# First layer of a split-float32 MLP: weight sums one pair ahead, activation sums on VectorE, two row tiles kept from PSUM, two bank tags

## The chip, the cores and the metric

One core of a Trainium2 chip runs the whole program. The metric is the device time of one execution in microseconds (us); smaller is better. The engines are TensorE (PE), VectorE (DVE), ScalarE (ACT), GpSimd (POOL) and SyncE (SP), of which the last only issues transfers here.

## The reference

One residual block over a sequence of 1024 rows with model width 1024: two kinds of attention, an output projection, and an MLP with squared relu. The change lies in the MLP's first layer and in what feeds it.

```python
        merged = gate_sb * (y_sb @ w_sb_out[l]) + gate_diff * (y_diff @ w_diff_out[l])
        x = x + rms_norm(merged @ w_o[l], g_post_mix[l])

        h = rms_norm(x, g_pre_mlp[l])
        u = jnp.square(jax.nn.relu(h @ w_up[l]))
        x = x + rms_norm(u @ w_down[l], g_post_mlp[l])
```

h is 1024 x 1024, u is 1024 x 4096, and everything is float32.

## The kernel before

**Products.** A float32 factor is split into a high and a low part (`split`, L606: ScalarE casts the high part at L607, VectorE subtracts to get the low part at L608), and a product takes three matmuls for each block of 128 rows. `product` (L755 to L767, matmul in L764) multiplies a 512-wide weight block with a page of h: 4 blocks x 3 = 12 matmuls of 128x512.

**First layer.** h is cut into a 2x2 arrangement of blocks, and the layer is done with seven block products instead of eight (Strassen's scheme in Winograd's form). The h pages are B11, B21, B22 and the differences T1 to T4. The weights come in 16 pairs of 128-column tiles (`up_pair(n)`, n = 0 to 15). For each pair, `sums` (L722) loads two tiles of `w_up` and GpSimd forms four sums of 128x512 (L726 to L729); `split_sums` then splits the results w1, w24, w32 into high and low parts. Pairs 4 to 15 also split the pair's own block wa and do seven products. For pairs 0 to 3 (AHEAD) the B11 and B21 products (`c11_0` to `c11_3`) are run ahead, before the other h pages exist; these pairs do five products later. VectorE adds the products out of PSUM (v, q, u12, u21, u22), ScalarE applies relu and square (`relu2`, L770 and L771). Then four activation sums us12 and us34 are formed on GpSimd (L866 to L869), and all seven parts are stored in DRAM for the second layer (L873; sums through SyncE's queue, the others through ScalarE's).

**What feeds it.** `finish_tile(t)`, t = 0 to 7, projects 128 rows, normalises them twice on ScalarE and VectorE (or_t, xr_t), transposes the result on TensorE (trh_t) and stores it in DRAM as h. Tile 7 alone goes from PSUM straight into the buffers `hraw`, as last 128 columns (LATE) of the blocks with c = 1; `load_h` reads the rest (EARLY, and the c = 0 blocks) back from DRAM when all tiles but 7 have been stored. The T pages are formed by subtractions of hraw on VectorE.

**Second layer.** It runs seven groups of products (L935), first A11 with B11: `load_a` reads activations, `load_b` weights of w_down, GpSimd subtracts weights (t, L900).

**Buffers and order.** Buffers come from pools with a fixed count for each tag: `row` 4, `raw` 2, `wide`, `tmp` 2, and two PSUM banks for each of the tags acc, sc, av, tr. A new tile of a tag waits until the last reader of the oldest one is done. Each engine executes its instructions in one fixed order, which a scheduler chooses at build time; each queue is in order too.

## Time and profile before

| | us |
|---|---|
| median of the runs | 1488.52 |
| fastest and slowest run | 1484.34, 1489.57 |
| the profiled execution | 1482.92 |
| its span, first to last instruction | 1481.2 |
| TensorE busy (matmuls) | 1442.6, 97% |
| VectorE busy | 959.9, 65% |
| ScalarE busy | 742.8, 50% |
| GpSimd busy | 406.4, 27% |

The page gives shares over the whole span. TensorE's gaps are short and lie in a few places, so the views by stretch and the timelines of single engines are of more use. In a timeline, a row is an instruction (or a run of like ones, with its count), and the bracket at its end gives how long the engine was idle before it and who released it.

### The profile page before, as it was taken

How to read it: one execution, taken by the hardware profiler on the slowest of the kernel's cores; microseconds unless marked ns; L12 is line 12 of the kernel's file. 1: busy time of each engine (PE TensorE's matmuls, PEld its weight loads, DVE VectorE, ACT ScalarE, POOL GpSimd, SP SyncE). 2: the span in 40 equal slices, each digit the busy share in tenths (PEclk: the TensorE clock that was granted, in tenths of full speed). 3: DMA queues.
4: the chain of work that ended last, by engine and by line, in shares of the span. 5: the costliest groups of instructions: out<-in, count | busy, mean ns of one | idle time of the engine just before them, and what ended most of it. 6: DMA issues, size and time to landing. Idle time of an engine off the chain costs nothing.

```text
span 1481.2 us, 20077 instructions
## 1 busy us (share of the span) xinstructions
PE 1442.6 (97%) x7302; PEld 1222.0 (83%) x7302; DVE 959.9 (65%) x1404; ACT 742.8 (50%) x1350; POOL 406.4 (27%) x376
## 2 busy tenths in 40 slices
PE   7999999999999999999999888999999999999997
PEld 6888998899889888888888766887888788888886
DVE  5487988898778857536554485444444489664783
ACT  6456666676556545744344363444445244534450
POOL 2022322230000000000001227655665557232611
PEclk9999999999999999999999999999999999999999
DMA  5342213222322344644367725344456585668671
GB/s 203 79 130 65 72 44 82 76 58 64 84 77 76 98 151 148 203 139 147 124 199 226 243 97 174 135 157 143 152 182 211 189 291 190 199 219 283 208 284 57
DMA packets 94459, 220.51 MB, mean 149 GB/s; under 512 B 9260, under 2 KB 25880, under 8 KB 94360
## 3 DMA queue, kind: packets, MB, share of 16 engines
q1 hardware_dynamic: 78904, 198.78, 41.6%
q10 hardware_dynamic: 15456, 20.45, 3.8%
q8 instruction: 57, 0.93, 0.3%
q14 instruction: 42, 0.34, 0.1%
HBM read 152.59 MB, written 60.57 MB: 144 GB/s over the span
## 4 chain that ended last, share of the span: by engine, by line
PE 80%; issue 7%; POOL 5%; DVE 3%; DMA 2%; ACT 1%; SPq 0%; POOLq 0%; DVEq 0%; ACTq 0%
PE dS L935 12%; PE dA L935 8%; PE o L656 6%; PE mix L567 6%; PE acc_gate L198 4%; PE acc_gate L196 4%; PE acc_gate L197 4%; PE c L764 3%; PE p_av L764 3%; PE p_tr L764 3%; PE z L263 2%; PE z L262 2%; PE tr_sb L281 2%; PE p_sc L764 1%; PE tr_df L281 1%
## 5 line engine op out<-in xcount | busy, mean ns | idle before, releaser
L331 DVE TENSOR_TENSOR_SCAN rest<-rest 128x896 f32<-128x896 f32 (+3 forms) x64 | 87.6, 1374 | 20.7 <-POOL rest L326 20.3
L198 PE MATMUL acc_gate<-h_hi,lo_gate 128*128 128x512 f32 x256 | 101.0, 394 | 0.0
L196 PE MATMUL acc_gate<-h_hi,hi_gate 128*128 128x512 f32 x256 | 100.8, 394 | 0.0
L197 PE MATMUL acc_gate<-h_lo,hi_gate 128*128 128x512 f32 x256 | 100.7, 393 | 0.0
L326 POOL TENSOR_SCALAR_AFFINE_SELECT rest<-rest 128x128 f32<-128x128 f32 x64 | 23.5, 367 | 240.5 <-ACT rest L322 223.8
L608 DVE TENSOR_TENSOR lS_lo<-raw_S,lS_hi 128x1024 fp32r<-128x1024 f32 x32 | 59.7, 1866 | 38.5 <-ACT lS_hi L607 38.3
L608 DVE TENSOR_TENSOR w_lo<-raw_up,w_hi 128x1024 fp32r<-128x1024 f32 x32 | 44.1, 1388 | 52.5 <-ACT w_hi L607 45.7
L935 PE MATMUL dS<-rT_hi,lS_hi 128*128 128x512 f32 x192 | 74.7, 389 | 0.0
L935 PE MATMUL dS<-rT_lo,lS_hi 128*128 128x512 f32 x192 | 74.7, 389 | 0.0
L935 PE MATMUL dS<-rT_hi,lS_lo 128*128 128x512 f32 x192 | 74.7, 389 | 0.0
L607 ACT CAST lS_hi<-raw_S 128x1024 fp32r<-128x1024 f32 x32 | 33.7, 1052 | 78.5 <-DMA raw_S<-s_dramS 50.0
L567 PE MATMUL mix<-y,hi_mix 128*128 128x512 f32 x256 | 68.6, 389 | 0.0
L116 POOL TENSOR_SCALAR rstd_o<-s 128x1 f32<-128x1 f32 x8 | 2.4, 299 | 239.7 <-DVE wa_lo L608 212.2
L394 ACT ACTIVATE s<-s,low 128x896 f32<-128x896 f32 (+7 forms) x64 | 49.6, 776 | 29.9 <-DVE low L389 29.7
L375 POOL MEMSET bias<- 64x64 f32 x4 | 0.6, 145 | 214.7 <-DMA bias<-bias_rows 154.6
L764 PE MATMUL c<-hB_hi,wa_hi 128*128 128x512 f32 x128 | 50.5, 395 | 7.8 <-ACT u L770 4.1
L389 DVE CUSTOM_DVE_ANT_0 s<-z,bias 128x512 f32<-128x512 f32 (+3 forms) x64 | 37.0, 587 | 32.3 <-PE z L263 26.4
L726 POOL TENSOR_TENSOR s<-raw_up 128x512 f32<-128x512 f32 x16 | 24.4, 1527 | 117.2 <-DMA raw_up<-in_w_up_dram 87.5
L567 PEld LDWEIGHTS mix<-y,hi_mix 128*128 128x128 f32 x256 | 48.0, 188 | 10.0
L198 PEld LDWEIGHTS acc_gate<-h_hi,lo_gate 128*128 128x128 f32 x256 | 48.1, 188 | 9.2
L770 ACT ACTIVATE u<-u 128x512 f32<-128x512 f32 x48 | 29.6, 628 | 51.9 <-DVE u L852 24.5
L197 PEld LDWEIGHTS acc_gate<-h_lo,hi_gate 128*128 128x128 f32 x256 | 48.2, 188 | 8.8
(339 smaller groups left out, 4871.4 us busy)
## 6 DMA issues: line engine op xcount, KB each, us to landing
raw_up<-in_w_up_dram SPq DMA_DIRECT2D x32, 512.0 KB, 4.2
s_dramS<-us SPq DMA_DIRECT2D x64, 256.0 KB, 2.5
raw_S<-s_dramS SPq DMA_DIRECT2D x32, 512.0 KB, 4.4
s_dramA<-u ACTq DMA_DIRECT2D x48, 256.0 KB, 2.6
raw_A<-s_dramA SPq DMA_DIRECT2D x24, 512.0 KB, 3.7
raw_gate<-in_w_in_dram SPq DMA_DIRECT2D x16, 512.0 KB, 3.7
gate_dram<-gt SPq DMA_DIRECT2D x32, 256.0 KB, 2.5
y<-y_dram SPq DMA_DIRECT2D x16, 512.0 KB, 7.0
```

The lines of the kernel that those rows point to most:

```text
L196: nc.tensor.matmul(acc, w_hi[:, ks], h_hi[k][:, cs], start=(k == 0), stop=False)
L197: nc.tensor.matmul(acc, w_hi[:, ks], h_lo[k][:, cs], start=False, stop=False)
L198: nc.tensor.matmul(acc, w_lo[:, ks], h_hi[k][:, cs], start=False, stop=(k == NK - 1))
L281: nc.tensor.transpose(tr[:, i * P:(i + 1) * P], w[qi][:, kb * P:(kb + 1) * P], ident)
L331: nc.vector.tensor_tensor_scan(back, back, back, 1.0, op0=ALU.mult, op1=ALU.bypass)
L389: nc.vector.tensor_tensor_reduce(out=s[:, c0:c1], in0=z, in1=bias[:, S - nk + c0:S - nk + c1], scale=1.0, scalar=BIG if prev is None else ...
L394: e = nc.scalar.activation(s[:, :nk], s[:, :nk], AF.Exp, bias=low, scale=-1.0, accum_out=sums[:, m:m + 1],)
L567: nc.tensor.matmul(accs[i][c], st[:, ks], mv[:, cs], start=(first and k % 4 == 0), stop=(last and k % 4 == 3),)
L608: nc.vector.tensor_tensor(lo, raw, f32(hi), op=ALU.subtract)
L656: nc.tensor.matmul(accs[n], st, mv[:, n * HALF:(n + 1) * HALF], start=(first and k == 0), stop=(last and k == NK - 1),)
L764: nc.tensor.matmul(acc, st[:, ks], mv, start=(first and k == 0 and i == 0), stop=(k == 3 and i == 2), skip_group_check=True,)
L935: nc.tensor.matmul(acc, st[:, e, ts], mv[:, e, :], start=(first and e == 0 and i == 0), stop=(last and e == 1 and i == 2))
```

## The change

1. `sums(n + 1)` is called in `up_pair(n)`, after the split of pair n's weights. Odd pairs load into two `row` tiles, even ones into two `raw` tiles as before.
2. The four activation sums go from GpSimd to VectorE; the third is placed ahead of the second.
3. Tile 6 goes from PSUM into `hraw` too, as tile 7 does; the transposes of tiles 6 and 7 and their copies come after `load_h`, which now leaves out 256 columns.
4. `c11_2` and `c11_3` use the bank tag "sc" instead of "acc".
5. Of the second layer's first two B11 weight blocks, one is loaded ahead into a `raw` tile, where two were loaded into `row` tiles.

```diff
-        if t == NT - 1:
-            load_h()
...
+        return partial(store_h, t, c, ts, o)
+
+    def store_h(t, c, ts, o):
...
-            if t == NT - 1:
+            if t >= NT - 2:
                 for q in range(2):
-                    nc.scalar.copy(hraw[j, 1, q][:, :, LATE], tr[:, q * 256:(q + 1) * 256].rearrange("p (k t) -> p k t", k=2))
+                    nc.scalar.copy(hraw[j, 1, q][:, :, ts], tr[:, q * 256:(q + 1) * 256].rearrange("p (k t) -> p k t", k=2))
...
+    FROM_DRAM = slice(0, HALF - 2 * P)
...
-                cs = EARLY if c else slice(0, HALF)
+                cs = FROM_DRAM if c else slice(0, HALF)
...
-    def sums(n, s1):
-        f0, f1 = (raw_up(2 * n + i, f"up{n}_{i}") for i in range(2))
+    def sums(n, s1=None):
+        if n % 2:
+            f0, f1 = (row(f"up{n}_{i}") for i in range(2))
+            for i, f in enumerate((f0, f1)):
+                nc.sync.dma_start(out=f, in_=w_up[2 * n + i])
+        else:
+            f0, f1 = (raw_up(2 * n + i, f"up{n}_{i}") for i in range(2))
+        if s1 is None:
+            s1 = row(f"s1_{n}", [P, HALF])
...
-        finish_tile(t)
+        finish = finish_tile(t)
+        if t < NT - 2:
+            finish()
+        elif t == NT - 2:
+            finish6 = finish
+        else:
+            load_h()
+            finish6()
+            finish()
...
-        accs = [bank("acc", f"c11_{2 * i + e}") for e in range(2)]
+        accs = [bank(BANKS[i % 2], f"c11_{2 * i + e}") for e in range(2)]
...
-        wa, w1, w24, w32 = weights0 if n == 0 else split_sums(*sums(n, row(f"s1_{n}", [P, HALF])))
+        wa, w1, w24, w32 = weights0 if n == 0 else split_sums(*summed)
+        summed = sums(n + 1) if n < UP - 1 else None
...
-        nc.gpsimd.tensor_tensor(s1, u12, u22, op=ALU.add)
-        nc.gpsimd.tensor_tensor(s2, s1, u11, op=ALU.subtract)
-        nc.gpsimd.tensor_tensor(s3, u11, u12, op=ALU.subtract)
-        nc.gpsimd.tensor_tensor(s4, u21, s2, op=ALU.subtract)
+        nc.vector.tensor_tensor(s1, u12, u22, op=ALU.add)
+        nc.vector.tensor_tensor(s3, u11, u12, op=ALU.subtract)
+        nc.vector.tensor_tensor(s2, s1, u11, op=ALU.subtract)
+        nc.vector.tensor_tensor(s4, u21, s2, op=ALU.subtract)
...
-            b11, b12 = first_b[pp] if pp < 2 else load_b(0, 0, pp, "a"), load_b(0, 1, pp, "a")
+            b11, b12 = first_b[0] if pp == 0 else load_b(0, 0, pp, "a"), load_b(0, 1, pp, "a")
...
-    first_b = [load_b(0, 0, pp, "a") for pp in range(2)]
+    first_b = [raw_tile("b00_first", [P, 2, HALF])]
+    nc.sync.dma_start(out=first_b[0], in_=wd[0, 0, 0])
```

TensorE, the products run ahead of the pairs. hB110 and hB111 are the halves of page B11, hB210 of B21; c11_i belongs to pair i. Before, the end of c11_0's first product and what follows it:

```order
L764 MATMUL c11_0_8928<-hB111_hi_8539,wa_lo0_8261 128x512
L764 MATMUL c11_1_8929<-hB110_hi_8537,wa_hi1_8266 128x512
L764 MATMUL c11_1_8929<-hB110_lo_8538,wa_hi1_8266 128x512
L764 MATMUL c11_1_8929<-hB110_hi_8537,wa_lo1_8267 128x512
L764 MATMUL c11_1_8929<-hB110_hi_8537,wa_hi1_8266 128x512
```

The same place after:

```order
L781 MATMUL c11_0_8926<-hB111_hi_8539,wa_lo0_8261 128x512
L781 MATMUL c11_2_8982<-hB110_hi_8537,wa_hi2_8272 128x512
L781 MATMUL c11_2_8982<-hB110_lo_8538,wa_hi2_8272 128x512
L781 MATMUL c11_2_8982<-hB110_hi_8537,wa_lo2_8273 128x512
L781 MATMUL c11_2_8982<-hB110_hi_8537,wa_hi2_8272 128x512
L781 MATMUL c11_2_8982<-hB110_lo_8538,wa_hi2_8272 128x512
L781 MATMUL c11_2_8982<-hB110_hi_8537,wa_lo2_8273 128x512
L781 MATMUL c11_2_8982<-hB111_hi_8539,wa_hi2_8272 128x512
L781 MATMUL c11_1_8927<-hB110_hi_8537,wa_hi1_8266 128x512
L781 MATMUL c11_1_8927<-hB110_lo_8538,wa_hi1_8266 128x512
```

Seven matmuls of c11_2 now stand between c11_0 and c11_1; before, c11_2 began only after both products of c11_0 and c11_1.

VectorE, around tile 7's last normalisation (or_7, the scalar-tensor-tensor that reads rstd_x27). hrawjcq is a block of h; L801 and L819 are the same subtraction. Before:

```order
L670 TENSOR_TENSOR or_7_8892<-o_7_1_8826,grow0_8169 128x512
L671 SCALAR_TENSOR_TENSOR xr_7_8891<-or_7_8892,rstd_o7_8897,xr_7_8891 128x1024
L676 SCALAR_TENSOR_TENSOR or_7_8892<-xr_7_8891,rstd_x27_8906,grow1_8171 128x1024
L801 TENSOR_TENSOR hraw000_8877<-hraw010_8875,hraw000_8877 128x2x384
L608 TENSOR_TENSOR hB220_lo_9052<-hraw110_8879,hB220_hi_9051 128x2x384
L803 TENSOR_TENSOR hraw010_8875<-hraw110_8879,hraw010_8875 128x2x384
```

After:

```order
L668 TENSOR_TENSOR or_7_8860<-o_7_1_8810,grow0_8169 128x512
L669 SCALAR_TENSOR_TENSOR xr_7_8859<-or_7_8860,rstd_o7_8865,xr_7_8859 128x1024
L819 TENSOR_TENSOR hraw000_8880<-hraw010_8878,hraw000_8880 128x2x384
L821 TENSOR_TENSOR hraw010_8878<-hraw110_8882,hraw010_8878 128x2x384
L819 TENSOR_TENSOR hraw001_8888<-hraw011_8886,hraw001_8888 128x2x384
L674 SCALAR_TENSOR_TENSOR or_7_8860<-xr_7_8859,rstd_x27_8874,grow1_8171 128x1024
L608 TENSOR_TENSOR hB220_lo_9050<-hraw110_8882,hB220_hi_9049 128x2x384
```

Three subtractions, one of them on a block of the second half (hraw001), have moved ahead of the normalisation that tile 7's transposes read.

GpSimd, sums of pairs 1 to 3 (s1_n and raw_up or up: weights; us12, us34: activations). Before:

```order
L728 TENSOR_TENSOR raw_up2_0_9336<-s1_2_9335,raw_up2_0_9336 128x512
L729 TENSOR_TENSOR raw_up2_0_9336<-raw_up2_0_9336 128x512
L866 TENSOR_TENSOR us12_1_9322<-u1_1_9241,u2_1_9242 128x512
L868 TENSOR_TENSOR us34_1_9323<-u11_0_8926,u1_1_9241 128x512
L867 TENSOR_TENSOR us12_1_9322<-us12_1_9322,u11_0_8926 128x512
L869 TENSOR_TENSOR us34_1_9323<-u2_1_9242,us12_1_9322 128x512
L726 TENSOR_TENSOR s1_3_9449<-raw_up3_1_9452 128x512
L727 TENSOR_TENSOR raw_up3_1_9452<-raw_up3_0_9450,raw_up3_1_9452 128x512
```

After:

```order
L737 TENSOR_TENSOR raw_up2_0_9239<-s1_2_9243,raw_up2_0_9239 128x512
L738 TENSOR_TENSOR raw_up2_0_9239<-raw_up2_0_9239 128x512
L735 TENSOR_TENSOR s1_3_9357<-up3_1_9354 128x512
L736 TENSOR_TENSOR up3_1_9354<-up3_0_9353,up3_1_9354 128x512
L737 TENSOR_TENSOR up3_0_9353<-s1_3_9357,up3_0_9353 128x512
L738 TENSOR_TENSOR up3_0_9353<-up3_0_9353 128x512
```

Between the weight sums of one pair and those of the next there is no longer an activation sum of the pair before.

## Rows read from the trace of the kernel before

**Rows 1.** Per-core line: span and mean granted TensorE clock
```profile
core 0: 1481.2 us, clock 0.995
```

**Rows 2.** Chain that ended last, in time order: start, us, what
```profile
836.80 3.41 DMA h_dram<-ht
...
1031.88 2.72 PE p_sc L764 x12
...
1172.10 3.89 DMA b_a<-in_w_down_dram
```

**Rows 3.** Stretches: length, busy PE, PEld, DVE, ACT, POOL, clock, DMA, GB/s
```profile
833.28:864.61 31.33, 24.81 (x114) 19.24 (x112) 20.46 (x30) 15.42 (x32) 2.37 (x6) 1.00 0.49 162
864.61:1016.93 152.32, 144.39 (x626) 116.13 (x624) 80.27 (x91) 70.08 (x108) 90.31 (x63) 1.00 0.43 147
1016.93:1028.97 12.04, 10.21 (x36) 7.95 (x37) 5.04 (x6) 5.65 (x8) 7.98 (x6) 0.86 0.53 172
1028.97:1156.94 127.97, 127.97 (x565) 105.81 (x564) 59.36 (x64) 60.07 (x89) 75.75 (x52) 1.00 0.54 182
1156.94:1182.33 25.39, 21.70 (x86) 17.44 (x85) 6.62 (x5) 8.29 (x12) 14.60 (x8) 0.87 0.47 175
1182.33:1481.20 298.87, 291.21 (x1285) 240.80 (x1283) 207.11 (x153) 119.43 (x147) 114.77 (x57) 0.99 0.64 217
```

**Rows 4.** Timeline of TensorE, row tile 7: start, us, line, operation, [idle before, releaser]
```profile
839.23 0.50 PE L764 MATMUL c<-hB_hi,wa_hi 128*128 128x512 f32 x1 [2.17 <-DVE or L670]
...
850.70 0.50 PE L764 MATMUL c<-hB_hi,wa_hi 128*128 128x512 f32 x1 [1.56 <-ACT u L770]
...
856.25 0.50 PE L764 MATMUL c<-hB_hi,wa_hi 128*128 128x512 f32 x1 [2.55 <-ACT u L770]
```

**Rows 5.** Timeline of SyncE's queue, ScalarE and VectorE, row tiles to pair 0
```profile
840.23 3.68 SPq L713 DMA_DIRECT2D hraw<-h_dram  x6
...
849.32 0.83 ACT L607 CAST hB_hi<-hraw 128x768 fp32r<-128x768 f32 x1 [6.38 <-DMA hraw<-h_dram]
...
842.97 1.29 DVE L676 SCALAR_TENSOR_TENSOR or<-xr,rstd_x,grow 128x1024 f32<-128x1024 f32 x1 [2.17 <-ACT p L784]
846.79 0.96 DVE L801 TENSOR_TENSOR hraw<-hraw,hraw 128x768 f32<-128x768 f32 x1 [2.53 <-DMA hraw<-h_dram]
...
864.02 0.69 DVE L608 TENSOR_TENSOR w<-s,w 128x512 fp32r<-128x512 f32 x1
```

**Rows 6.** Waits, 833 to 1183: who, for whom, us, times, longest
```profile
DVE u L852 <- POOL us L867: 12.4, 6, 2.3
...
PE p_sc L764 <- ACT w_hi L607: 3.9, 3, 1.6
...
PE p_sc L764 <- DVE w_lo L608: 2.2, 3, 1.0
```

**Rows 7.** Timeline of GpSimd, sums of pairs 1 and 3
```profile
872.73 3.29 POOL L726 TENSOR_TENSOR s<-raw_up 128x512 f32<-128x512 f32 x1 [29.80 <-DMA s_dramA<-u]
...
908.04 1.29 POOL L726 TENSOR_TENSOR s<-raw_up 128x512 f32<-128x512 f32 x1 [4.01 <-DMA raw_up<-in_w_up_dram]
```

**Rows 8.** Timeline of TensorE, end of pair 8
```profile
1016.93 0.50 PE L764 MATMUL c<-hB_hi,wa_hi 128*128 128x512 f32 x1 [1.28 <-ACT p L846]
...
1024.52 0.50 PE L764 MATMUL p_av<-hB_hi,w_hi 128*128 128x512 f32 x1 [1.83 <-DVE u L852]
```

**Rows 9.** Timeline of GpSimd, SyncE's queue, ScalarE, TensorE, second layer's start
```profile
1169.68 4.72 POOL L900 TENSOR_TENSOR t<-b_a,b_a 128x1024 f32<-128x1024 f32 x2
...
1172.10 3.21 SPq L891 DMA_DIRECT2D b_a<-in_w_down_dram  x4
...
1176.02 1.04 ACT L607 CAST rB_hi<-b_a 128x1024 fp32r<-128x1024 f32 x1 [10.40 <-DMA b_a<-in_w_down_dram]
...
1177.11 2.08 PE L935 MATMUL dA<-rB_hi,lA_hi 128*128 128x512 f32 x4 [3.69 <-ACT rB_hi L607]
```

**Rows 10.** Busy by stretch, columns as in rows 3: four pairs at full pace
```profile
1040.00:1116.16 76.16, 76.16 (x338) 62.91 (x337) 33.59 (x37) 35.80 (x53) 48.61 (x35) 1.00 0.49 167
```

More of the change, by code (lines that the diff above doesn't have):

```diff
@@ L754, in hybrid_block_kernel @@
         if t == 4:
-            sums0 = sums(0, stream.tile([P, HALF], F32, tag="tmp", name="s1_0", bufs=1))
+            summed = sums(0, stream.tile([P, HALF], F32, tag="tmp", name="s1_0", bufs=1))
     def product(acc, a, b, first=True):
@@ L788, in hybrid_block_kernel @@
             state.append((p1s[i][:, e, :], u11s[i][:, e, :]))
-    weights0 = split_sums(*sums0)
+    weights0 = split_sums(*summed)
+    summed = None
     for name, make in (("B22", big_pair), ("T2", big_pair), ("T1", pair_page), ("T3", pair_page), ("T4", pair_page)):
@@ L817, in up_pair @@
     def up_pair(n):
+        nonlocal summed
         ahead = n < AHEAD
-        wa, w1, w24, w32 = weights0 if n == 0 else split_sums(*sums(n, row(f"s1_{n}", [P, HALF])))
+        wa, w1, w24, w32 = weights0 if n == 0 else split_sums(*summed)
+        summed = sums(n + 1) if n < UP - 1 else None
         u1, u2 = wide(f"u1_{n}"), wide(f"u2_{n}")
```

## The prediction

> **What bounds the kernel now.** The per-core line comes first [rows 1]: the span is 1481.2 us and the mean granted clock 0.995, so TensorE is the engine that sets the time almost everywhere. The chain of waits gives its pace [rows 2]: twelve matmuls, which is one product of the first layer, take 2.72 us at full clock. The third view is the busy time by stretch from the last row tiles of h to the end [rows 3]. The reader is to compare each stretch with its products at 2.72 us.
>
> - 833.28 to 864.61 (the last two row tiles, the products run ahead): 31.33 us, TensorE busy 24.81, so 6.5 idle.
> - 864.61 to 1016.93 (pairs 0 to 7, four products of 8): some 624 matmuls, 52 products, 141.4 us at pace; it took 152.32, so 10.9 lost.
> - 1016.93 to 1028.97 (end of pair 8): three products, 8.2 us; it took 12.04, so 3.9 lost, with a granted clock of 0.86.
> - 1028.97 to 1156.94 (pairs 9 to 15): 47 products, 127.8 us of 127.97. Nothing is lost.
> - 1156.94 to 1182.33 (end of pair 15, start of the second layer): 84 matmuls, 19.0 us, of 25.39, so 6.35 lost, clock 0.87.
> - After 1182.33 TensorE is busy for 291.21 of 298.87 us, on work that the change does not touch.
>
> The sum, 27.7 us, is the most that the change can win in these stretches. It is 1.9% of the time.
>
> **The change part by part.** *Transition.* The idle 6.5 us are four gaps, three of them in [rows 4] and the fourth 0.2. The 2.17 at 839.23 is the first product waiting for an "acc" bank that VectorE still reads for tile 7. The 1.56 and 2.55 are c11_2 and c11_3 waiting for ScalarE's relu to leave the same two banks. With banks "sc" for c11_2 and c11_3 the last two gaps and the 0.2 have no cause left: 4.3 us. In the new order seven matmuls of c11_2 stand ahead of c11_1 and cover 7 x 0.227 = 1.6 of the 2.17. So TensorE alone would reach pair 0 some 5.9 us earlier, near 858.7.
>
> Whether pair 0's operands are there then is VectorE's matter. Before, its first subtraction of h starts at 846.79 and the first split weight of pair 0 ends at 864.02 + 0.69 = 864.7 [rows 5]: 17.9 us, 2.4 of it waiting for the cast that ScalarE began at 849.32, after 6.38 us of waiting for the same loads. The loads were issued at 840.23 because tile 6's store, 836.80 + 3.41 in the chain [rows 2], had to land first. Tile 6 no longer goes through DRAM, so the loads can go at least 840.2 - 836.8 = 3.4 us earlier, and about 5 if the copies that fed the store are counted too. VectorE then begins at 841.8 to 843.4. One thing is added to its queue: three subtractions of h now stand ahead of tile 7's last normalisation (it is the order shown in the section on the change), which is queued for the third h block, and behind which tile 7's transposes and TensorE wait. The normalisation itself is 1.29 us of VectorE (842.97) between subtractions. Ends: 841.8 + 15.5 = 857.3 and 843.4 + 1.3 + 17.9 = 862.6. Only the first gives the whole 5.9, the second gives 2.0. I take 859, near the early end, since the row of 846.79 waited for a DMA and nothing else: gain 5.5, range 2.0 to 6.5. The two added copies of tile 6 on ScalarE replace two copies and two stores; they cost nothing while ScalarE is busy 15.42 of 31.33 us [rows 3].
>
> *Pairs 0 to 7.* TensorE waits here for weights: 3.9 us for the cast high part, 2.2 us for the low part [rows 6], the rest as shorter restarts. They come late because GpSimd makes a pair's four sums only as that pair begins, after its load (idle 4.01 us before 908.04 [rows 7]), and in the same queue as four activation sums of the pair before. The change gives GpSimd four operations instead of eight, one pair ahead of use: 4 x 1.29 = 5.2 us of work with 13.6 us (five products) or 19.04 us (seven) to do it in. A load of 4 us and a split (cast 1.0 us, subtraction about twice 0.69, an estimate) fit too. One place remains: the sums of pair 1 cannot begin until VectorE has finished with an h block whose row they use, and they then run beside a full VectorE, where the sum at 872.73 took 3.29 instead of 1.29. Pair 1 begins 13.6 us after pair 0, near 872.6; sums begun near 864.7, as the last h split before the weights ends, and three operations long (3.3 + 1.3 + 1.3), with cast and subtraction (2.4), are ready at 873. I take 0.4 for that and 1.0 for a second place of the kind, 1.4 us in all, ends 0 and 5 (three sums at 3.29: 864.7 + 9.9 + 2.4 = 877). Gain 10.9 - 1.4 = 9.5, range 5.9 to 10.9.
>
> *VectorE's new load.* Four sums of 128x512 at 0.69 us [rows 5] are 2.8 us a pair. In four pairs at full pace VectorE was busy 33.59 us, 8.4 a pair, and TensorE idle for none of 76.16 [rows 10]. So 11.2 of 19.04 us in pairs 4 to 15, and, without the split of the pair's own block (1.4), 9.8 of 13.6 in pairs 0 to 3. VectorE also no longer waits for GpSimd's sums to free a buffer, 12.4 us in six places [rows 6]. I count the four sums at nothing: what covers them is TensorE's own work, and if a bank's reader came late they would cost the 1.83 us shown below.
>
> *Pair 8.* The gaps are 1.28 and 1.83 [rows 8]; the second ends on VectorE's u, the operation that waited for GpSimd's sums in [rows 6]. After it the granted clock drops (0.86 over the stretch, between the 2.4 and the 1.2 GHz level). Without GpSimd's sums in that path neither has a cause: gain 3.9, range 1.3 (one gap and the clock stay) to 3.9.
>
> *Pairs 9 to 15* have nothing to give: 0.
>
> *Start of the second layer.* TensorE idles 3.69 us at 1177.11 for the split of a block of w_down, whose load was issued at 1172.10, when GpSimd's t (L900), begun at 1169.68 with two operations in 4.72 us, had read a row and freed it [rows 9]. The load took 3.89 [rows 2], the cast 1.04. In the new code one of the first two blocks lies in a raw buffer, so one more row is free and the block that was late is loaded already. The next one is late instead: its row comes free after the second t, 1174.4; load 3.9 and cast 1.0 bring it to 1179.3, or 1180 if the cast queues. TensorE wants it one block (24 matmuls, 5.4 us) after it wanted the former, 1173.4 + 5.4 = 1178.8. The new gap is 0.5 to 1.4 us, of which I take the larger, and perhaps 0.5 by the clock. The activation block that shares the raw buffers is now loaded one at a time; if they come that late, the whole 6.35 stays lost. Gain 6.35 - 1.9 = 4.4, range 0 to 6.3.
>
> Sum: 5.5 + 9.5 + 3.9 + 0 + 4.4 = 23.3 us. The profiled execution took 1482.92, so it would take 1459.6. The runs of before have a median of 1488.52, 5.6 above the profiled one, and their fastest is 1.4 above it. By the median the same sum gives 1465.2; I take 1464, nearer to the median.
>
> **The rivals.** *VectorE and GpSimd hold each other up.* That the sum at 872.73 took 3.29 us beside a full VectorE and that at 908.04 took 1.29 [rows 7] says that they can. If each of the four weight sums stops VectorE for its 1.29 us, VectorE has 9.8 + 5.2 = 15.0 us to do in the 13.6 of pairs 0 to 3, 1.4 too many, 5.6 over four pairs; from pair 4 on 16.4 of 19.04 still fit. The gain is 23.3 - 5.6 = 17.7, the time 1470. With the second layer's start as late as before (4.4 more) it is 1474. For it: two-input sums join VectorE. Against it: GpSimd's own work halves.
> The Trainium skill, page "SBUF — State Buffer", section "Who interferes with whom", states this as a rule that speaks against the change: a VectorE instruction with two SBUF inputs and a GpSimd instruction that reads SBUF exclude each other, and the loser stands still for the whole instruction. The trace agrees in GpSimd's 3.29 us against 1.29; that VectorE loses as often is not shown in these rows.
>
> *The waits are handed on.* The h blocks come no earlier (a row buffer is freed late rather than the store), tile 7's normalisation queued behind them holds the transposes, so the transition gains 0, and pairs 0 to 7 gain only the 3.9 + 2.2 us of [rows 6]. Then the change does not do what it says, and the gain is about 6: 1482. Against it: pairs 9 to 15 have the same sums and lose nothing [rows 3].
>
> *Slower.* The moved sums stand in VectorE's in-order queue. The last one of pair n-1 needs ScalarE's square of that pair's last block; queued behind it are the evictions of pair n, and TensorE waits for their banks. Before, one late u cost TensorE 1.83 us and the clock [rows 8]. In pairs 4 to 15 the bank that q (L850) reads is filled by the third product, 8.2 us into a pair, and accumulated onto again from 13.6 us; with its own 0.69 q is done near 9, so it decides from some 4 us of delay. To end over 0.5% slower it has to eat 23.3 + 7.4 us over 12 pairs, 2.6 us each beyond that margin: 1496. Against it: 7.8 us of VectorE's 19.04 are free.
>
> **How the numbers follow.** Forecast about 1464 with the ranges above: 0.68. The port rival, 1470 to 1474: 0.17. Handed on, near 1482: 0.10. Slower, 1496: 0.05. Half a per cent, 7.4 us, is about what a measurement of this kernel can tell from no change: below 1481 is faster (0.68 and 0.17, less 0.02 for the tail), 1481 to 1496 the same (0.11), above it slower (0.06, the mechanism above and a little for what was not thought of). The low end: all 27.7 us from 1484 give 1456. The high end takes in the port rival with the lower bound of one more part: 1477.
>
> **What would show it right or wrong.** In the profile after: no TensorE gap on ScalarE's relu between 840 and 858, and pair 0 beginning near 859. GpSimd's sums of pair n+1 beginning while pair n runs, and no wait of a product for a split weight over 0.5 us beyond pair 1. No gap and no clock below 1.00 at pair 8. The gap in the second layer one block later and under 1.5 us. VectorE at 11 to 12 us a pair in pairs 9 to 15, with TensorE busy throughout. The prediction is wrong if TensorE waits for VectorE's evictions in the pairs, if VectorE's 0.69 us grow to 2 beside GpSimd, if tile 7's transposes wait for an h block, or if the first activation blocks of the second layer are what TensorE waits for.

## The result and the profile after

The changed kernel takes 1466.69 us (median of four runs, 1465.43 to 1468.61), the kernel before 1486.47 (four runs; the median of 1488.52 that the prediction starts from was that of three of them); the ratio is 0.9866, with a 95% interval of 0.9841 to 0.9891. The gain is 19.8 us by the medians and 16.8 us between the two profiled executions (1482.92 and 1466.14). The prediction was 1464, with a range of 1456 to 1477 and a sum of 23.3 us against the profiled execution.

The busy time by stretch of the changed kernel, cut at the same places of TensorE's work as in [rows 3] (first product run ahead; pair 0; fifth product of pair 8; pair 9; second group of the second layer; end). Columns as there.

```profile
833.57:860.87 27.30, 24.50 (x114) 19.31 (x112) 20.52 (x31) 15.51 (x34) 3.55 (x6) 1.00 0.57 187
860.87:1006.99 146.12, 143.26 (x625) 116.65 (x625) 119.21 (x124) 72.18 (x109) 60.61 (x38) 1.00 0.51 166
1006.99:1015.15 8.16, 8.16 (x37) 6.76 (x36) 4.37 (x5) 4.53 (x7) 2.85 (x3) 1.00 0.33 119
1015.15:1195.60 180.45, 177.68 (x782) 146.17 (x780) 113.17 (x112) 78.19 (x110) 51.17 (x29) 1.00 0.57 191
1195.60:1464.40 268.80, 261.28 (x1153) 216.10 (x1151) 182.49 (x141) 108.55 (x136) 102.65 (x52) 0.99 0.63 208
```

For the fourth stretch the kernel before has, in one piece from pair 9 to the same second group:

```profile
1028.97:1212.26 183.29, 179.60 (x782) 148.03 (x781) 91.06 (x81) 79.31 (x111) 106.01 (x65) 0.98 0.57 197
```

So the four stretches gave 31.33 - 27.30 = 4.0, 152.32 - 146.12 = 6.2, 12.04 - 8.16 = 3.9 and 183.29 - 180.45 = 2.8 us, 16.9 in all; the prediction had 5.5, 9.5, 3.9 and 4.4. The granted clock is 1.00 in all four. Products alone, in the first stretch with the 16 transposes of tiles 6 and 7, would take some 23.3, 141.4, 8.2 and 176.8 us at 2.72 each, so 4.0, 4.7, 0 and 3.6 us are still lost. Where, TensorE's timeline shows (start, us, operation, in brackets its idle time and who ended it):

```profile
847.81 1.06 PE L682 MATMUL trh<-ident,or 128*128 128x128 f32 x8 [1.83 <-DVE or L674]
858.01 0.50 PE L781 MATMUL c<-hB_hi,wa_hi 128*128 128x512 f32 x1 [0.95 <-ACT p L801]
872.26 0.50 PE L781 MATMUL p_tr<-hT_lo,w_hi 128*128 128x512 f32 x1 [0.89 <-DVE hT_lo L608]
930.68 0.50 PE L781 MATMUL c<-hB_hi,wa_hi 128*128 128x512 f32 x1 [1.09 <-ACT p L866]
1166.45 1.19 PE L955 MATMUL dA<-rB_hi,lA_hi 128*128 128x512 f32 x4 [1.54 <-ACT rB_hi L607]
1174.38 0.50 PE L955 MATMUL dA<-rB_lo,lA_hi 128*128 128x512 f32 x1 [1.17 <-DVE rB_lo L608]
```

Two more waits for hT_lo (0.42 and 0.15) and one of 0.27 in pair 4 are left out. Three things are new or larger than before. Tile 7's transposes wait for its normalisation on VectorE (or, L674). Pair 0 waits for VectorE's splits of the h pages. And VectorE's and GpSimd's operations have become longer where they meet. VectorE's timeline of the changed kernel, columns as above:

```profile
845.51 0.96 DVE L819 TENSOR_TENSOR hraw<-hraw,hraw 128x768 f32<-128x768 f32 x1 [5.28 <-DMA hraw<-h_dram]
846.39 1.28 DVE L674 SCALAR_TENSOR_TENSOR or<-xr,rstd_x,grow 128x1024 f32<-128x1024 f32 x1
...
865.22 10.15 DVE L608 TENSOR_TENSOR hT_lo<-hraw,hT_hi 128x768 fp32r<-128x768 f32 x9
...
879.16 0.68 DVE L856 TENSOR_TENSOR u<-p_av,q 128x512 f32<-128x512 f32 x1
...
883.11 1.77 DVE L886 TENSOR_TENSOR us<-u,u 128x512 f32<-128x512 f32 x1
```

GpSimd's timeline of the changed kernel, in the same time:

```profile
866.64 1.89 POOL L735 TENSOR_TENSOR s<-up 128x512 f32<-128x512 f32 x1 [25.68 <-DVE hT_lo L608]
...
878.16 2.25 POOL L736 TENSOR_TENSOR raw_up<-raw_up,raw_up 128x512 f32<-128x512 f32 x1
...
884.30 1.74 POOL L735 TENSOR_TENSOR s<-up 128x512 f32<-128x512 f32 x1
```

The normalisation starts when the subtraction ahead of it ends, which waited 5.28 us for the third h block. The moved activation sum takes 1.77 us, not the 0.69 at which it was priced, and the weight sum next to it 1.74 instead of 1.29. Of the 64 moved sums 18 take more than 1 us, up to 1.79; the other 46 take 0.70 at most. VectorE's 84 additions that read one input from a PSUM bank (v, q and u) are not held up: all take 0.67 to 0.69 us, 28 of them beside a sum of GpSimd, as the one at 879.16 beside that at 878.16.

### The profile page after: what moved, and what is told of

It is laid out like the page before. It is cut to its first block, busy times and chain, and to the rows that moved or that the text cites. A ratio compares the mean times of both kernels' runs of the same rounds, so it can differ in the third digit from the quotient of the medians.

```text
span 1464.4 us, 20068 instructions
## 1 busy us (share of the span) xinstructions
PE 1437.3 (98%) x7302; PEld 1219.3 (83%) x7302; DVE 1021.1 (70%) x1468; ACT 743.2 (51%) x1352; POOL 322.4 (22%) x312
## 5 line engine op out<-in xcount | busy, mean ns | idle before, releaser
L196 PEld LDWEIGHTS acc_gate<-h_hi,hi_gate 128*128 128x128 f32 x256 | 48.2, 188 | 8.6
L608 DVE TENSOR_TENSOR lA_lo<-raw_A,lA_hi 128x1024 fp32r<-128x1024 f32 x24 | 37.5, 1561 | 24.9 <-ACT lA_hi L607 23.3
L287 ACT CAST wth_sb<-tr_sb 128x512 fp32r<-128x512 f32 (+1 forms) x80 | 41.2, 548 | 26.5 <-PE tr_sb L281 25.1
L326 POOL TENSOR_SCALAR_AFFINE_SELECT beta<-beta 128x128 f32<-128x128 f32 x64 | 53.7, 838 | 3.2 <-ACT beta L323 2.1
L288 DVE TENSOR_TENSOR wtl_sb<-tr_sb,wth_sb 128x512 fp32r<-128x512 f32 (+1 forms) x80 | 48.5, 627 | 7.7 <-ACT wth_sb L287 7.5
```

The source lines that it names most:

```text
L196: nc.tensor.matmul(acc, w_hi[:, ks], h_hi[k][:, cs], start=(k == 0), stop=False)
L287: nc.scalar.copy(hi[:, :n], tr[:, :n])
L288: nc.vector.tensor_tensor(lo[:, :n], tr[:, :n], f32(hi[:, :n]), op=ALU.subtract)
L326: nc.gpsimd.affine_select(tl[:, dg], tl[:, dg], pattern=[[-1, P]], compare_op=ALU.is_gt, fill=fill, base=0, channel_multiplier=1,)
L608: nc.vector.tensor_tensor(lo, raw, f32(hi), op=ALU.subtract)
```

## The experiments

Each is the changed kernel with one thing altered. The table has the four stretches in us (S1 products run ahead to pair 0, S2 to the fifth product of pair 8, S3 to pair 9, S4 to the second layer's second group), read from TensorE's starts in each timeline, and the time of the runs. A time marked (one) is a single execution, the others are medians of four to six. The first product run ahead starts anywhere from 833.2 to 837.5 us in these executions, and the same kernel has 833.85 in v0123 and 835.77 in v0123_t; so a single execution's total tells little below 4 us, and the stretches are what is compared. They spread too: these two executions of one kernel differ by 0.7 us in S1, 0.01 in S2 and 1.8 in S4, and the runs whose edit lies ahead of the second layer (e_one_tag, e_tile6, e_no_wsums and those from g_one on) have 179.5 to 182.3 us in S4.

| run | S1 | S2 | S3 | S4 | time |
|---|---|---|---|---|---|
| before | 31.33 | 152.32 | 12.04 | 183.29 | 1486.47 |
| changed | 27.30 | 146.12 | 8.16 | 180.45 | 1466.69 |
| e_us_pool | 28.32 | 148.17 | 8.16 | 185.19 | 1473.55 (one) |
| e_own_pair | 27.80 | 151.38 | 8.16 | 180.13 | 1473.19 (one) |
| e_tile6 | 27.74 | 148.24 | 8.17 | 180.24 | 1468.26 (one) |
| e_one_tag | 27.54 | 145.95 | 8.16 | 180.18 | 1465.89 (one) |
| e_first_b2 | 27.16 | 146.06 | 8.17 | 179.37 | 1466.50 (one) |
| e_no_wsums | 22.75 | 141.50 | 8.16 | 180.71 | 1457.63 (one) |
| g_one | 27.63 | 145.86 | 8.16 | 182.33 | 1467.73 |
| g_q1 | 28.27 | 145.30 | 8.16 | 181.37 | 1467.67 |
| v0 | 26.55 | 146.24 | 8.16 | 180.45 | 1466.01 |
| v01 | 26.94 | 143.37 | 8.16 | 181.51 | 1463.81 |
| v0123 | 26.77 | 142.95 | 8.16 | 179.52 | 1461.82 (one) |
| v0123_t | 27.44 | 142.94 | 8.16 | 181.29 | 1463.86 |

**Activation sums back on GpSimd** (e_us_pool).

```diff
-        nc.vector.tensor_tensor(s1, u12, u22, op=ALU.add)
+        nc.gpsimd.tensor_tensor(s1, u12, u22, op=ALU.add)
...
```

> The changed kernel with one part undone: the four activation sums of a pair are on GpSimd again. Stages of the changed kernel, by TensorE's starts: 27.3 us from the first product run ahead to pair 0, 146.3 from there to the fifth product of pair 8, 8.2 from there to pair 9, 180.4 from there to the second layer's second group. Theory A (the prediction's: GpSimd's eight operations a pair and the wait of VectorE's u for them are what cost): the second stage goes back up by 3 us or more, to 149 to 152, and the third to about 12, with the clock below 1.00. Rival B (the weight sums made one pair ahead are enough, since 8 x 1.29 us fit in a pair; VectorE and GpSimd only block each other now): second stage 146 or less, down to 144, third stage 8.2.

S2 rose by 2.1 us, less than A's 3 and more than B allows, and S3 stayed at 8.16, against A. S1's 1.0 us more lies ahead of the sums: after a wait of 2.35 us for tile 7's normalisation some eight matmuls started 0.43 us apart instead of 0.227, and the granted clock of the stretch fell to 0.94. The busy time by stretch in this run, for S1:

```profile
833.17:861.49 28.32, 25.59 (x113) 20.65 (x112) 20.66 (x31) 15.79 (x36) 3.85 (x6) 0.94 0.55 183
```

The larger loss, 4.7 us, was in S4, which neither theory named: GpSimd has to finish pair 15's sums before it makes the second layer's first weight difference (t, L920), and TensorE then waits 4.38 us. GpSimd's timeline in this run:

```profile
1160.72 1.29 POOL L889 TENSOR_TENSOR us<-u,us 128x512 f32<-128x512 f32 x1
1161.96 2.39 POOL L920 TENSOR_TENSOR t<-b_a,raw_b_first 128x1024 f32<-128x1024 f32 x1
```

GpSimd's timeline in the changed kernel, the same operation:

```profile
1155.65 2.92 POOL L920 TENSOR_TENSOR t<-b_a,raw_b_first 128x1024 f32<-128x1024 f32 x1 [44.02 <-DVE us L888]
```

TensorE's timeline in this run, the wait that follows:

```profile
1171.96 2.07 PE L955 MATMUL dA<-rB_hi,lA_hi 128*128 128x512 f32 x4 [4.38 <-ACT rB_hi L607]
```

The last eviction of pair 15 starts at 1155.31 here and at 1152.18 in the changed kernel, so t begins 6.65 us after it here and 3.47 there.

**Weight sums in their own pair** (e_own_pair).

```diff
-        wa, w1, w24, w32 = weights0 if n == 0 else split_sums(*summed)
-        summed = sums(n + 1) if n < UP - 1 else None
+        wa, w1, w24, w32 = weights0 if n == 0 else split_sums(*sums(n, row(f"s1_{n}", [P, HALF])))
...
```

> The changed kernel with the weight sums made in their own pair again, in two raw buffers (and the second layer's first two weight blocks in row buffers again, without which two raw buffers do not do). Theory A (the weights that come late are made late): the second stage, 146.3 us in the changed kernel and 152.3 before, goes to 150 or more, with TensorE waiting for the cast or the low part of a weight as before, 5 us or more of it. Rival B (taking the activation sums off GpSimd was enough): it stays within 1 us of 146.3. The start of the second layer is disturbed in either case by up to 3 us.

A by the stretch: S2 is 151.4 us, 5.3 more, and TensorE waits again for the cast of a weight. These waits add up to 3.5 us, less than A's 5; another 4.1 are waits for VectorE's u and q. GpSimd idles 8.01 us for the load before the sums of a pair. S3 stayed at 8.16: for pair 8 either move is enough. GpSimd's timeline in this run:

```profile
886.68 1.29 POOL L735 TENSOR_TENSOR s<-raw_up 128x512 f32<-128x512 f32 x1 [8.01 <-DMA raw_up<-in_w_up_dram]
```

TensorE's timeline in this run:

```profile
909.70 0.50 PE L781 MATMUL p_sc<-hT_hi,w_hi 128*128 128x512 f32 x1 [1.51 <-ACT w_hi L607]
```

**Tile 6 through DRAM** (e_tile6).

```diff
-            if t >= NT - 2:
+            if t == NT - 1:
...
-    FROM_DRAM = slice(0, HALF - 2 * P)
+    FROM_DRAM = EARLY
...
```

> The changed kernel with tile 6 of h stored in DRAM and read back again (the order of the loads stays as in the changed kernel). Theory A (the h blocks come early because tile 6's store is no longer waited for): VectorE's first subtraction of h starts near 846, not 838, pair 0 begins 4 to 5 us later, 27.3 us becomes 31 to 33. Rival B (the row buffers, free only when tile 6's rows are done, set the time of the h loads): 27.3 us becomes 28 to 29, the third h block comes within 1 us of the 845.5 that it had.

Both missed. VectorE's first subtraction came even later than A said, at 849.91, but S1 grew by only 0.4 us: the order of VectorE's work differs, with fewer page splits ahead of pair 0's weights, and TensorE then waits 1.88 us inside pair 0 for the low part of one (S2 2.1 more). TensorE's timeline in this run:

```profile
864.01 0.79 PE L776 MATMUL p_sc<-hT_hi,w_lo 128*128 128x512 f32 x1 [1.88 <-DVE w_lo L608]
```

The busy time by stretch in this run, from the start of pair 0:

```profile
860.94:870.00 9.06, 7.18 (x23) 5.51 (x24) 9.06 (x15) 9.06 (x17) 0.00 (x0) 0.81 0.55 175
```

The part is worth 2.6 us over both stretches in this execution. The waits alone do not make it: TensorE's gaps in S2 add up to 3.2 us, 2.8 in the changed kernel. After that wait some seven matmuls start 0.43 us apart instead of 0.227, with a granted clock of 0.81, which is some 1.4 us (an estimate from these spacings).

**One bank tag for the products run ahead** (e_one_tag).

```diff
-        accs = [bank(BANKS[i % 2], f"c11_{2 * i + e}") for e in range(2)]
+        accs = [bank("acc", f"c11_{2 * i + e}") for e in range(2)]
```

> The changed kernel with all four products run ahead in the two acc banks again. Theory A (the banks were what TensorE waited for, 2.17 + 0.24 + 1.56 + 2.55 us before): TensorE waits again for VectorE's reading of tile 7 and twice for the relu, 4 us or more in all, and 27.3 us becomes 30 to 32. Rival B (VectorE's chain of h pages sets when pair 0 begins, the banks only fill the time): the gaps come back but pair 0 begins within 1 us of where it did, 27.3 becomes 28 at most.

B, and more than that: even the waits mostly stay away. TensorE waits 0.80 us for a relu and 0.50 for a copy, 0.95 and no relu in the changed kernel, and pair 0 begins where it did. TensorE's timeline in this run:

```profile
851.95 0.50 PE L781 MATMUL c<-hB_hi,wa_hi 128*128 128x512 f32 x1 [0.80 <-ACT u L787]
855.48 0.50 PE L781 MATMUL c<-hB_hi,wa_hi 128*128 128x512 f32 x1 [0.50 <-ACT p L801]
```

Two banks are thus enough in the changed kernel. What four would have done to the waits of 1.56 and 2.55 us in [rows 4], in the kernel before, was not run. The relus that these name were late themselves: on ScalarE the first stood right behind the cast at 849.32 that waited 6.38 us for an h block [rows 5], the second behind more casts and copies of h. With the blocks earlier the relu comes almost in time in two banks.

**Two row buffers for the second layer's first blocks** (e_first_b2).

```diff
-    first_b = [raw_tile("b00_first", [P, 2, HALF])]
-    nc.sync.dma_start(out=first_b[0], in_=wd[0, 0, 0])
+    first_b = [load_b(0, 0, pp, "a") for pp in range(2)]
```

> The changed kernel with the second layer's first two weight blocks loaded into row buffers again. Theory A (one row more is free, so the wait at the start of the second layer goes one block further and shrinks): the stretch from pair 9 to the second group, 180.4 us, becomes 182 to 184, with one wait of 3 us or more. Rival B (the four sums that left GpSimd shorten the start of the second layer, not the buffer): it stays within 0.7 us of 180.4.

S4 became 1.1 us shorter, outside both but within its spread. TensorE's timeline in this run, its first wait there:

```profile
1161.60 1.19 PE L955 MATMUL dA<-rB_hi,lA_hi 128*128 128x512 f32 x4 [0.69 <-ACT rB_hi L607]
```

It is 0.69 us, and 0.63 in e_own_pair, which has these row buffers too; with the raw buffer and the sums on VectorE it is 1.06 to 2.26 in ten runs. So the raw buffer gained nothing, and this wait is longer with it. That it takes a place from the activation blocks, as the prediction had feared, would fit but is not shown.

**No weight sums** (e_no_wsums).

```diff
-        nc.gpsimd.tensor_tensor(s1, a21, a22, op=ALU.add)
...
-        return n, wa, s1, f0, f1
+        return n, wa, a21, f0, f1
...
```

> The changed kernel without the four weight sums of each pair (64 operations on GpSimd left out; the raw blocks are split in their place), so that GpSimd has nothing to do beside VectorE in the first layer. In the changed kernel VectorE's nine splits of h pages from 865.2 take 10.15 us and some of its sums 1.78 instead of 0.69; TensorE waits 0.89 + 0.42 + 0.15 us for those splits and 0.27 + 1.09 in pair 4. Theory A (the two engines exclude each other): the nine splits take some 5 us (three of 0.87, six of 0.42), all activation sums 0.69, and these five waits go, 146.3 us becomes 141.5 to 143. Rival B (VectorE has too much work, whatever GpSimd does): the splits still take 8 us or more, TensorE's waits for them stay above 1 us.

A, and S2 is at its floor: 141.50 us. The nine splits take 5.77 us where they took 10.15. VectorE in this run:

```profile
841.46 0.96 DVE L813 TENSOR_TENSOR hraw<-hraw,hraw 128x768 f32<-128x768 f32 x1 [1.47 <-DMA hraw<-h_dram]
...
860.79 5.77 DVE L608 TENSOR_TENSOR hT_lo<-hraw,hT_hi 128x768 fp32r<-128x768 f32 x9
```

Not expected was S1: 22.75 us, no wait of TensorE left, and the third subtraction of h, which needs the "third h block" of the prediction, at 841.5 instead of 845.5. Like for like S1 is 23.5, 3.8 us shorter: tile 6's eight transposes, 0.8 us, come ahead of its first product in this run. The eight h loads are issued in 4.57 us instead of 11.56. SyncE's queue in this run:

```profile
830.79 4.57 SPq L715 DMA_DIRECT2D hraw<-h_dram  x8
```

SyncE's queue in the changed kernel:

```profile
829.89 11.56 SPq L715 DMA_DIRECT2D hraw<-h_dram  x8
```

The changed kernel's GpSimd makes pair 0's sums while it should compute tile 6's reciprocal root, and VectorE idles 5.00 us for that root. So tile 6's row is stored late, and until the store has landed its row buffer, which one of the last two h loads needs, is occupied: SyncE's queue stands for 7.0 us. Its waits in the changed kernel, 822 to 862 (who, for whom, us, times, longest):

```profile
SPq L715 <- DMA x_dram<-xr: 7.0, 1, 7.0
```

Some 5 of these 7.0 us are the store itself (an estimate, 7.6 - 2.6). Issued at 832.31 among six h loads (829.89 to 832.9), it takes 7.6 us to land. The DMA issues of the changed kernel at that time (what, engine, count, size, us to landing):

```profile
x_dram<-xr ACTq DMA_DIRECT2D x1, 512.0 KB, 7.6
```

The same store in the kernel before, where those loads are issued 8 us after it:

```profile
x_dram<-xr ACTq DMA_DIRECT2D x1, 512.0 KB, 2.6
```

It takes 2.7 us in e_no_wsums, ahead of the loads too. GpSimd's timeline of the changed kernel:

```profile
823.85 2.08 POOL L735 TENSOR_TENSOR s<-raw_up 128x512 f32<-128x512 f32 x1 [0.39 <-DMA raw_up<-in_w_up_dram]
```

VectorE's timeline of the changed kernel:

```profile
830.99 1.28 DVE L669 SCALAR_TENSOR_TENSOR xr<-or,rstd_o,xr 128x1024 f32<-128x1024 f32 x1 [5.00 <-POOL rstd_o L117]
```

**One or three subtractions of h on GpSimd** (g_one, shown, and g_q1, with all three of the loop); q is the half.

```diff
-            nc.vector.tensor_tensor(b11, b12, b11, op=ALU.subtract)
+            eng = nc.gpsimd if q else nc.vector
+            eng.tensor_tensor(b11, b12, b11, op=ALU.subtract)
```

> The changed kernel with one of the subtractions of h, that of the second half's first block (the one that stands ahead of tile 7's normalisation and waits 5.28 us for its DMA), moved to GpSimd, which is idle there. Theory A (VectorE's in-order queue held the normalisation and with it tile 7's transposes): TensorE's wait of 1.83 us for it goes, VectorE does some 4 us of other h work in that time, pair 0 begins 2 to 3 us earlier (27.3 becomes 24.5 to 25.5) and the waits of 1.46 us for the splits shrink; in all 2 to 4 us less than the changed kernel. Rival B (the subtraction takes about 2 us on GpSimd and blocks VectorE, and the second half's pages come later by that): 27.3 becomes 26.5 at best, no gain in all.

> As the run before it, with all three subtractions of the second half's blocks on GpSimd. Theory A (the engines exclude each other): GpSimd's six operations of about 2 and 0.7 us take the place of 4 us of VectorE's and block it as long: no better than moving one, by 0 to 2 us worse. Rival B (VectorE's amount of work is what counts): 3 us or more better than moving one.

In g_one the wait of 1.83 us went as A said, but S1 did not shrink (27.63): TensorE now waits 1.08 and 1.51 us for ScalarE's copies of finished products, which stand behind casts of the late h blocks. No gain, so the normalisation's place in VectorE's queue alone does not set S1; it was the first wait to show. TensorE's timeline in g_one:

```profile
853.41 0.50 PE L781 MATMUL c<-hB_hi,wa_hi 128*128 128x512 f32 x1 [1.08 <-ACT p L801]
857.93 0.50 PE L781 MATMUL c<-hB_hi,wa_hi 128*128 128x512 f32 x1 [1.51 <-ACT p L801]
```

g_q1 is no better (S1 28.27, after a wait of 2.68 us and with a granted clock of 0.94; S2 0.6 less; 1467.67 us), as A of its expectation says.

**Pair 0's sums on VectorE** (v0), **of pairs 0 and 1** (v01), **of pairs 0 to 3** (v0123, and v0123_t timed).

```diff
+        eng = nc.vector if n == 0 else nc.gpsimd
-        nc.gpsimd.tensor_tensor(s1, a21, a22, op=ALU.add)
+        eng.tensor_tensor(s1, a21, a22, op=ALU.add)
...
```

with n < 2 and n < 4 in the others.

> The changed kernel with the four weight sums of pair 0 alone moved from GpSimd to VectorE. In the changed kernel and before, GpSimd does these sums from 823.8 to 830.4, in the same queue ahead of the reciprocal root for tile 6, and VectorE waits 5.00 us for that root; without any weight sums tile 6 was done 6 us earlier and the stretch to pair 0 took 22.75 us instead of 27.3. Theory A (this queue on GpSimd delays tile 6, with it the row buffers, the h loads and pair 0): VectorE's wait for the root goes, the h loads are issued within 6 us instead of 11.6, the stretch to pair 0 becomes 23 to 24.5, 3 to 4 us less in all. Rival B (the h loads' own time on the DMA queues, 3 MB, sets it, and the run without sums won by the order of its instructions): the loads still end near 845 and the stretch stays above 26.

The wait for the root went and the loads are issued in 4.20 us, but they start at 834.57, 4.7 us later, when tile 5's store has landed. The third block is there at 845.84, and S1 is 26.55: B by its numbers. Tile 5 is late on ScalarE. VectorE's normalisation of it is only 1.1 us later than in the changed kernel and its transposes 0.3, but ScalarE's copies of them, which feed the store, now stand behind tile 6's mean square in its queue. ScalarE's timeline in v0:

```profile
830.23 1.06 ACT L108 ACTIVATE or<-xr 128x1024 f32<-128x1024 f32 x1 [6.49 <-DVE xr L669]
...
831.29 1.05 ACT L688 COPY ht<-trh 128x512 f32<-128x512 f32 x2
```

ScalarE's timeline in the changed kernel, the same copies:

```profile
826.29 1.08 ACT L688 COPY ht<-trh 128x512 f32<-128x512 f32 x2 [2.63 <-PE trh L682]
```

SyncE's queue in v0:

```profile
834.57 4.20 SPq L715 DMA_DIRECT2D hraw<-h_dram  x8
```

VectorE's timeline in v0:

```profile
845.84 0.96 DVE L820 TENSOR_TENSOR hraw<-hraw,hraw 128x768 f32<-128x768 f32 x1 [1.58 <-DMA hraw<-h_dram]
```

From the first issue to the third block these loads take 11.3 us here and 10.7 in e_no_wsums; the changed kernel, issuing at 829.89, takes 15.6 because of the rows. So v0 took away one delay of the loads and, by the new order on ScalarE, brought another; it does not settle between A and B. That an early tile 5 and an early tile 6 together make the 3.8 us of e_no_wsums was not tried.

> As the run before it, with the four weight sums of pair 1 on VectorE too. Theory A (a sum on GpSimd next to a full VectorE costs VectorE as much time as it lasts there, so that four sums at 0.69 on VectorE itself are cheaper): the nine splits of h pages, 10.15 us in the changed kernel, take 6 to 8 us with the sums between them, TensorE's waits in pairs 0 and 1 fall below 1 us, 1 to 2 us better than the run before it. Rival B (more work in VectorE's queue ahead of what TensorE waits for): waits for the low parts of pair 1's weights of 1 us or more, no better or up to 3 us worse.

> As the run before it, with the weight sums of pairs 0 to 3 all on VectorE. Theory A: VectorE has some 12.6 of 13.6 us a pair to do in pairs 1 to 3 and TensorE waits for it little; the wait of 1.09 us in pair 4 goes; within 1.5 us of the run before it. Rival B (VectorE then is the bound): TensorE waits 4 us or more in pairs 1 to 4 for VectorE's results.

> The kernel of the run before it (weight sums of pairs 0 to 3 on VectorE) once more, now timed in rounds. Its one execution took 1461.82 us, with 143.0 us from pair 0 to the fifth product of pair 8, where the changed kernel had 146.1 and products alone take 141.4. Theory A (GpSimd's sums next to a full VectorE were the dearer place): the stretch is 143 us again, within 0.5, and the median 1460 to 1464, 3 to 5 us below the changed kernel's 1466.69, at a ratio to the kernel before of 0.982 to 0.985. Rival B (the one execution was a lucky one in the stages before): the stretch differs, or the median is 1465 or more.

A in all three by its mechanism. S2 falls to 143.37 and 142.95 us, and to 142.94 when run again, against 146.12. In v0123 GpSimd works 37.51 us in that stretch instead of 60.61, and although VectorE makes 12 more operations there, it is busy 114.72 us instead of 119.21 (busy time by stretch, v0123):

```profile
860.62:1003.57 142.95, 142.47 (x625) 117.03 (x625) 114.72 (x136) 71.54 (x109) 37.51 (x26) 1.00 0.52 170
```

Sums of 0.68 us between the splits, which take their 0.87 and 0.42 again, replace sums of 1.3 to 2.3 us that stopped them. In all, v0123_t takes 1463.86 us at a ratio of 0.9857 (0.9834 to 0.9880); the interval overlaps that of the changed kernel, so the 3.2 us are shown in the stretch and not in the total. The ratio misses its expectation of 0.982 to 0.985 by a little, and so do the 2.8 us by the medians (3 to 5 expected); the kernel before took 1484.70 in that set of runs.

## Why the prediction was right or wrong

**Direction and range** held: faster, 1466.69 in 1456 to 1477. The sum was 6.4 us too large, in three of its terms. That the forecast is only 2.7 us off is luck in part: the sum was taken from a median of three runs, 2 us above that of four; from the profiled execution it gave 1459.6, against 1466.14. One of the prediction's own signs of being wrong came about, tile 7's transposes waiting for an h block (1.83 us), and another nearly, VectorE's 0.69 us growing to 2 beside GpSimd (1.79).

**Transition, 5.5 expected, 4.0 measured; the step that failed is the first one,** where 4.3 us of waits were given to the two banks. e_one_tag shows that the tags are worth nothing once the other parts are in (27.54 against 27.30). The releaser named in [rows 4] was an instruction that itself stood in a queue, and the row of ScalarE's 6.38 us wait, quoted in the next paragraph, held the first of the two up. The next step, h blocks earlier because of tile 6's store, was right (VectorE's first subtraction starts at 838.23, before 841.8), and e_tile6 sizes it at 2.6 us, in part by the clock. What it left out is who else holds the last blocks: tile 6's row buffers, late because pair 0's sums stand ahead of a reciprocal root on GpSimd, in both kernels, and later still in the changed one, where their store is under way among the h loads. The text named the danger (the normalisation queued for the third block) and then chose the early end for a reason, one row that waits for a DMA, that says nothing on the third block. It is the mechanism of the rival "the waits are handed on" (0.10), at a smaller price: TensorE waits 1.83 us there, not the whole term.

**Pairs 0 to 7, 9.5 expected, 6.2 measured.** The mechanism was right: e_own_pair gives back 5.3 us and e_us_pool 2.1. The 1.4 us that were to stay are 4.7, and they are GpSimd's sums beside VectorE: without them the stretch is at 141.5, and with those of pairs 0 to 3 on VectorE at 142.95. The mis-sized term is the price of the activation sums, which were counted at 0.69 us and hidden. They take up to 1.79 next to GpSimd, and the splits in pair 0 take 10.15 instead of 5.77. This is the rival "VectorE and GpSimd hold each other up", which had 0.17 and 5.6 us; it happened, with TensorE's waits in pairs 0 and 4, and cost 3.3 us more than was allowed. The rule of the Trainium skill, page "SBUF — State Buffer", section "Who interferes with whom", is borne out on the side that was open: VectorE loses as well, 0.69 to 1.77 us for one operation. The kernel before had rows of it that the prediction did not read: 15 of its 16 splits of s take 1.10 to 1.28 us there, where the row of 864.02 has 0.69. In steady state it is harmless: VectorE is busy 12.6 us a pair (50.44 over four pairs, 11.2 expected) and TensorE idles for none of 76.16 (busy time by stretch, the changed kernel):

```profile
1034.35:1110.51 76.16, 76.16 (x338) 63.06 (x337) 50.44 (x53) 34.82 (x53) 23.25 (x18) 1.00 0.48 159
```

**Pair 8, 3.9 expected and measured.** One refinement: either move of sums is enough for it, as e_us_pool and e_own_pair both have 8.16.

**Pairs 9 to 15, 0 expected and measured.**

**Start of the second layer, 4.4 expected, 2.8 measured; the step that failed is its mechanism.** It kept t (L900 before, L920 after) at 1169.68 [rows 9] and gave the gain to the buffer. But t stood right behind four GpSimd sums of 1.29 us, which the change takes off GpSimd. The chain of waits of the kernel before goes through them:

```profile
1167.07 1.29 POOL us L867
...
1169.68 2.41 POOL t L900
```

Undoing that part costs 4.7 us there, more than S4's spread; undoing the buffer costs nothing. The size is less sure, since S4 spreads by 2.8 us. Of the 2.8 us, 1.0 are shorter waits (3.69 against 1.54 + 1.17); about 2 are the clock, as ten matmuls after the wait of 3.69 start 0.43 us apart instead of 0.227, and none in the changed kernel.

**Nearly additive:** over S1 and S2, in single executions, undoing one part costs 5.8 us (sums ahead; with the buffer), 3.1 (sums to VectorE), 2.6 (tile 6), 0.1 (tags) and -0.2 (buffer), 11.4 together where the whole change gives 10.2.

**Still open:** what remains in S1 (4 us) is shown to go in e_no_wsums, but that run also changes the order of instructions on several engines; neither of the two partial remedies (g_one, v0) isolates it. The late row of tile 6 is seen in the queue; what it costs is not shown.

## What to carry to other kernels

A wait names the instruction that ended it; before it is priced, look at what stood ahead of that instruction in its own queue, since the remedy belongs there. When work moves between VectorE and GpSimd, price it as if the two shared one resource for operations with two inputs in SBUF, and look at what the emptied engine does next: here the largest gain of moving the activation sums was at the one place, the start of the next layer, where GpSimd's next work was awaited. Undoing the parts one by one showed in five runs that two of five were worth nothing beside the others. And read an added wait together with the matmuls behind it, since in several runs the clock cost as much as the wait.

## What the runs showed of the hardware

A VectorE operation of 0.69 us (two inputs in SBUF) takes up to 1.79 next to GpSimd's sums, and the twelve sums that GpSimd makes from 866.64 on take 1.35 to 2.25 us instead of 1.29: both lose. Which of them loses differs. In the kernel before, the same nine splits keep the 5.77 us that they take alone, and GpSimd's sum that starts beside them takes 3.29 [rows 7]. VectorE's timeline of the kernel before:

```profile
869.10 5.77 DVE L608 TENSOR_TENSOR hT_lo<-hraw,hT_hi 128x768 fp32r<-128x768 f32 x9
```

VectorE's additions with one input in PSUM keep their 0.69 us beside GpSimd. In the second layer VectorE's split of 1.23 us takes 3.42 beside GpSimd's operations of 2.4 to 3.4. Four sums on VectorE itself (2.7 us) are cheaper for a full VectorE than the same sums on GpSimd beside it, as its busy time in v0123 shows.

The clock kept its higher level (2.4 GHz) through all of the changed kernel's first layer, with single gaps of up to 1.83 us. After the gap of 4.38 us in e_us_pool four matmuls took 2.07 us, as after the 3.69 us in [rows 9], which is the lower level (1.2 GHz); after the gap of 1.54 us at the same place in the changed kernel four took 1.19. The length of a gap alone did not decide it: after the 2.35 us in e_us_pool the granted clock fell, and after 2.40 us at the same place in v0123_t it stayed at 1.00.

A store of 512 KB took 2.6 us from issue to landing ahead of the h loads, and 7.6 when issued among six of them.
